# Differential attention's scores in one row-half stretch, and priorities from pool mixer to cross-attention

## The chip, the cores and the metric

The kernel runs on one core of a Trainium2 chip. TensorE (PE in the profile) multiplies matrices: it loads a stationary operand (a weight load, PEld) and streams columns past it into a bank of PSUM, the accumulator memory. VectorE (DVE), ScalarE (ACT) and GpSimd (POOL) work on the elements, SyncE (SP) and POOL issue the transfers (DMA). Each engine runs its own instructions in their order; semaphores make one wait for another. The metric is device microseconds of one execution; less is better.

## The reference, cut to what matters

Two decoder layers over 512 tokens of 1024 features. Each layer: half-step SwiGLU feed-forward, token mixer, cross-attention into 256 memory tokens, second half-step feed-forward, each followed by a residual layer norm. The mixer of layer 0 is differential attention, that of layer 1 a causal pooling mixer.

```python
def block(args):                       # differential attention, 128 queries
    qblk, i = args
    s = jnp.einsum('bqhcd,bkhcd->bhcqk', qblk, k).astype(jnp.float32) * scale
    qpos = i * DA_QBLOCK + jnp.arange(DA_QBLOCK)
    mask = kpos[None, :] <= qpos[:, None]
    s = jnp.where(mask, s, jnp.finfo(jnp.float32).min)
    p = jax.nn.softmax(s, axis=-1)
    a = p[:, :, 0] - lam * p[:, :, 1]
    return jnp.einsum('bhqk,bkhe->bqhe', a.astype(v.dtype), v)
...
for i in range(DEPTH):
    m, j = i % N_MIXERS, i // N_MIXERS
    x = layer_norm(a * x + 0.5 * swiglu_ffn(x, ffn_w_in[i, 0], ffn_w_out[i, 0]), ln_g[i, 0], ln_b[i, 0])
    ...                                # h: differential attention or pool mixer
    x = layer_norm(a * x + h, ln_g[i, 1], ln_b[i, 1])
    x = layer_norm(a * x + memory_cross_attention(x, mem, xa_wq[i], xa_wkv[i], xa_wo[i]), ln_g[i, 2], ln_b[i, 2])
    ...
```

There are eight heads. A head has two maps (c = 0, 1) with 64 features each for queries and keys, and 128 features for values. Query block i of 128 tokens sees (i + 1) x 128 keys.

## The kernel before, in words

**Numbers.** Every float32 operand is split into a high part and a low rest, both in a 32-bit format that TensorE reads fast. A product is three matrix products: high by high, low by high, high by low. `split` makes the high part on ScalarE and the rest on VectorE; `mm3` issues the three products and returns an estimated time, 3 x max(107, 0.42 x columns) ns, which drives the weaving below.

**Order.** The program is written as a sequence of instructions; a planner lays it out on the engines ahead of time. Among instructions that it holds ready on an engine it takes the one written first, unless a block is under `high_priority`. `issue_after` and `after` put an instruction behind a named one of its engine. `weave` runs a main generator and a side generator: the main one reports the estimated time of its products, and when that time reaches the gap (900 ns here) times the weight that the side last returned, the side may write its next step. `WAIT` makes the side ask again.

**Differential attention (`diff_attention`).** Main (`da_main`) projects queries and keys of each head (`q`, `k`; 24 products of 512 columns each) and, per two heads, values (`v`), then multiplies the first four heads' results by the output weights. Side (`da_side`) does the attention itself, in four blocks of queries a head. Step s writes the scores of block s (`da_scores`), the mixture of block s - 1 (`da_mix`), its transposes for block s - 2 (`da_turn`), the output of block s - 3 (`da_out`), and, at the end of a head, the scale (`da_scale`) and its turn (`da_turn_out`). A head's scores may begin 6000 ns of main time after its keys are written.

**Scores.** Queries and keys of a head lie as 128 rows: map 0 in rows 0 to 63, map 1 in rows 64 to 127. For blocks 0 and 1, `da_key` copies the first 256 keys on ScalarE into tiles that hold zeros in the other half's rows (`low`, line 1139), so that one product with all 128 rows yields both maps side by side (line 1154). For blocks 2 and 3 each map is a product of 64 rows, alternating between the halves (line 1159). Per map, VectorE masks and reduces (line 1164) and ScalarE takes the exponential (line 1167).

**Banks.** [...] Two (`mm`) serve the projections; six (`aux`: px, py, yz, two each) rotate through the scores, transposes and outputs. The output of two blocks shares a bank: ScalarE copies a part out (line 1205), VectorE adds the other (line 1206), and two squares on ScalarE write into the bank again as scratch (line 1209).

**Pool mixer to cross-attention (layer 1).** `pool_mixer` splits the tokens, pools them by band matrices (`pp`), multiplies by group weights (`ps`) and ends with the layer norm (`ln_token`: square on ScalarE, line 379, variance, line 380, power on POOL, line 381, two passes on VectorE, lines 383 and 385). It is the side of a weave whose main part (`early_kv`) computes keys and values of the memory for the first heads of cross-attention (`pk`, `pv`). Its first keys' weights come from `cols`, whose splits appear under lines 125 and 126. `xa_main` then projects the queries (`xq`) in two halves of 256 tokens, because the last tokens' transposes (`turn_late`, `pt`, line 496) come late.

Of the kernel before, what the change touches and what calls it, by code (L numbers as in the profile page):

```python
# [9 lines left out]
F32 = mybir.dt.float32  # L10
# [7 lines left out]
P = 128  # L18
D = 1024
S = 512  # L20
# [18 lines left out]
W_SC, W_T, W_O, W_E = (1.1, 1.4, 1.8, 2.2), (0.5, 0.7, 0.9, 1.1), (0.4, 0.8, 0.6, 1.1), (0.6, 0.8)  # L39
LM, LT, LO, LS = 1, 2, 3, 5  # L40
# [69 lines left out]
class Trunk:  # L110
# [1020 lines left out]
    def da_key(self, ps):  # L1131


        k, t = self.pair("qk"), self.da_rope(ps)
        apart = self.keys_apart[len(self.heads) % 2]
        self.split(k[0], k[1], t)
        for whole, part in zip(k, apart):
            for m, rows in enumerate(HALVES):
                self.nc.scalar.copy(part[rows, m], whole[rows, : 2 * P].bitcast(F32))
        return k, apart  # L1140

    def da_scores(self, st, i):

        nc = self.nc
        q, k, n = st["q"], st["k"], (i + 1) * P
        qi, kn = slice(i * P, n), slice(0, n)
        mx, rc, cf = self.small("mx"), self.small("rc", (P, 1)), self.small("cf", (P, 1))
        sm = st["sm"][:, i]
        mm, terms = nc.tensor.matmul, ((0, 0), (1, 0), (0, 1))
        if i < 2:  # L1150
            both = self.aux("sc")[:, : 2 * n].rearrange("p (m n) -> p m n", m=2)
            sc = [both[:, m] for m in range(2)]
            for a, b in terms:
                mm(both, q[a][:, qi], k[1][b][:, :, kn], start=a == b, stop=b == 1)
        else:
            sc = [self.aux("sc")[:, :n] for m in range(2)]
            for a, b in terms:
                for m, rows in enumerate(HALVES):
                    mm(sc[m], q[a][rows, qi], k[0][b][rows, kn], start=a == b, stop=b == 1)
        p = [self.tmp("p")[:, :n] for m in range(2)]  # L1160
        with self.tc.high_priority():
            for m in range(2):
                least = mx[:, m : m + 1]
                nc.vector.tensor_tensor_reduce(
                    p[m], sc[m], self.mask[:, S - n :], -1.0, -NEG, ALU.add, ALU.min, least
                )
                nc.scalar.activation(
                    p[m], p[m], AF.Exp, bias=least, scale=-1.0, accum_out=sm[:, m : m + 1]
                )
        st["m", i] = p, sm, rc, cf  # L1170
# [93 lines left out]
    def da_side(self):  # L1264

        n = DA_H * NT
        for s in range(n + LS + 2):
            h, i = divmod(s, NT)
            if s < n:
                while h >= len(self.heads) or self.clock < self.heads[h][0] + LEAD:  # L1270
                    yield WAIT
                self.da_scores(self.heads[h][1], i)
                yield W_SC[i]
            h, i = divmod(s - LM, NT)
            if 0 <= s - LM < n:
                self.da_mix(self.heads[h][1], i)
            h, i = divmod(s - LT, NT)
            if 0 <= s - LT < n:
                self.da_turn(self.heads[h][1], i)
                yield W_T[i]  # L1280
            h, i = divmod(s - LO, NT)
            if 0 <= s - LO < n:
                while len(self.heads[h][1]["v"]) < NT:
                    yield WAIT
                self.da_out(self.heads[h][1], i)
                yield W_O[i]
            h, i = divmod(s - LS, NT)
            if 0 <= s - LS < n and i == NT - 1:
                self.da_scale(self.heads[h][1])
                yield W_E[0]  # L1290
            h, i = divmod(s - LS - 1, NT)
            if 0 <= s - LS - 1 < n and i == NT - 1:
                self.oT[h] = self.da_turn_out(self.heads[h][1])
                yield W_E[1]

    def diff_attention(self, layer, ln):
        self.keys_apart = [self.pair("low", (P, 2, 2 * P)) for i in range(2)]
        for pair in self.keys_apart:
            for t in pair:
                for m, rows in enumerate(HALVES):  # L1300
                    self.nc.gpsimd.memset(t[rows, 1 - m].bitcast(F32), 0.0)
# [56 lines left out]
    def pool_mixer(self, layer, ln):  # L1358
# [39 lines left out]
        for t in range(NT):  # L1398
# [17 lines left out]
            self.ln_token(t)  # L1416
# [344 lines left out]
```

## Time and profile before

| | |
|---|---|
| Median of three runs | 1916.96 us (1916.87 to 1918.63) |
| Profiled execution, its own time | 1915.99 us |
| Its span, first to last instruction | 1914.2 us |
| TensorE busy | 1898.0 us, 99% |
| VectorE, ScalarE, GpSimd busy | 1551.7, 1016.6, 319.3 us |
| Mean granted TensorE clock | 0.999 |
| Differential attention | some 344 to 555 us of the span |
| Pool mixer to the first queries of cross-attention | some 1386 to 1460 us |

Rows in order of time give start, duration, engine, line, operation, output <- inputs, the operands' shape, how many were merged, and in brackets how long the engine stood idle before and what released it. Matrix products overlap in the array, so a row's duration is longer than the time after which the next one starts; what a product costs is read from start to start. In the rows that group instructions, the numbers after the bar are total busy time, mean ns of one, and idle time just before them.

### The profile page before, as it was taken

How to read it: one execution, taken by the hardware profiler on the slowest of the kernel's cores; microseconds unless marked ns; L12 is line 12 of the kernel's file. 1: busy time of each engine (PE TensorE's matmuls, PEld its weight loads, DVE VectorE, ACT ScalarE, POOL GpSimd, SP SyncE). 2: the span in 40 equal slices, each digit the busy share in tenths (PEclk: the TensorE clock that was granted, in tenths of full speed). 3: DMA queues.
4: the chain of work that ended last, by engine and by line, in shares of the span. 5: the costliest groups of instructions: out<-in, count | busy, mean ns of one | idle time of the engine just before them, and what ended most of it. 6: DMA issues, size and time to landing. Idle time of an engine off the chain costs nothing.

```text
span 1914.2 us, 32507 instructions
## 1 busy us (share of the span) xinstructions
PE 1898.0 (99%) x13088; PEld 1732.0 (90%) x13088; DVE 1551.7 (81%) x2250; ACT 1016.6 (53%) x1578; POOL 319.3 (17%) x282
## 2 busy tenths in 40 slices
PE   9999999999999999999999999999999999999998
PEld 8999998888879888999998999999898889999996
DVE  7888889888867558889888988898787568998886
ACT  6555454566745435655553655555455436555552
POOL 3112121111110002221220311212130012211210
PEclk9999999999999999999999999999999999999999
DMA  9978772332225317987785687878344438867861
GB/s 249 215 176 177 177 139 78 91 89 67 89 67 161 116 60 194 193 175 164 143 191 171 117 180 166 181 164 186 101 132 133 137 84 174 178 156 168 189 130 54
DMA packets 246743, 277.96 MB, mean 145 GB/s; under 512 B 8256, under 2 KB 212544, under 8 KB 246592
## 3 DMA queue, kind: packets, MB, share of 16 engines
q0 software_dynamic: 92928, 92.29, 31.5%
q1 hardware_dynamic: 153664, 183.59, 29.9%
q8 instruction: 103, 1.69, 0.4%
q14 instruction: 48, 0.39, 0.1%
HBM read 273.75 MB, written 2.10 MB: 144 GB/s over the span
## 4 chain that ended last, share of the span: by engine, by line
PE 82%; DVE 11%; ACT 3%; DMA 2%; issue 1%; POOL 1%; SPq 0%; DVEq 0%; ACTq 0%; POOLq 0%
PE x L210 7%; PE x L211 7%; PE x L212 7%; PE z L210 4%; PE z L211 4%; PE z L212 4%; PE ps L210 4%; PE ps L212 4%; PE ps L211 4%; PE px L212 2%; PE px L210 2%; PE px L211 2%; PE y L212 2%; PE y L210 2%; PE y L211 2%; PE pz L212 1%
## 5 line engine op out<-in xcount | busy, mean ns | idle before, releaser
L715 POOL DMA_DIRECT2D ra<-in_ffn_w_in_dram x132 | 170.8, 1316 | 981.8 <-DVE wl L722 966.2
L720 ACT CAST wh<-ra 128x1024 fp32r<-128x1024 f32 x176 | 185.1, 1054 | 206.9 <-PE x L211 65.7
L722 DVE TENSOR_TENSOR wl<-ra,wh 128x1024 fp32r<-128x1024 f32 x176 | 214.2, 1222 | 66.5 <-ACT wh L720 66.1
L210 PE MATMUL x<-xe,wh 128*128 128x256 f32 x704 | 194.8, 277 | 0.0
L211 PE MATMUL x<-xe,wh 128*128 128x256 f32 x704 | 194.6, 276 | 0.0
L212 PE MATMUL x<-xe,wl 128*128 128x256 f32 x704 | 194.5, 276 | 0.0
L720 ACT CAST wh<-rc 128x1024 fp32r<-128x1024 f32 x132 | 138.9, 1053 | 101.6 <-PE x L211 41.4
L125 ACT CAST wh<-b 128x1024 fp32r<-128x1024 f32 x112 | 117.8, 1051 | 130.5 <-PE x L211 67.2
L722 DVE TENSOR_TENSOR wl<-rc,wh 128x1024 fp32r<-128x1024 f32 x132 | 160.0, 1220 | 24.9 <-ACT wh L720 24.9
L126 DVE TENSOR_TENSOR wl<-b,wh 128x1024 fp32r<-128x1024 f32 x112 | 136.8, 1221 | 40.2 <-ACT wh L125 40.2
L210 PE MATMUL x<-xh,wh 128*128 128x256 f32 x536 | 148.5, 277 | 0.0
L211 PE MATMUL x<-xl,wh 128*128 128x256 f32 x536 | 148.2, 276 | 0.0
L212 PE MATMUL x<-xh,wl 128*128 128x256 f32 x536 | 148.2, 276 | 0.0
L211 PEld LDWEIGHTS x<-xe,wh 128*128 128x128 f32 x704 | 132.3, 188 | 1.4
L210 PEld LDWEIGHTS x<-xe,wh 128*128 128x128 f32 x704 | 132.1, 188 | 1.3
L212 PEld LDWEIGHTS x<-xe,wl 128*128 128x128 f32 x704 | 132.2, 188 | 0.0
L126 DVE TENSOR_TENSOR wl<-raw,wh 128x1024 fp32r<-128x1024 f32 x64 | 82.2, 1288 | 42.0 <-ACT wh L125 41.2
L211 PEld LDWEIGHTS x<-xl,wh 128*128 128x128 f32 x536 | 100.7, 188 | 0.7
L210 PEld LDWEIGHTS x<-xh,wh 128*128 128x128 f32 x536 | 100.6, 188 | 0.7
L212 PEld LDWEIGHTS x<-xh,wl 128*128 128x128 f32 x536 | 100.6, 188 | 0.0
L125 ACT CAST wh<-raw 128x1024 fp32r<-128x1024 f32 x64 | 66.4, 1048 | 60.6 <-PE xq L211 20.2
L210 PE MATMUL z<-xe,wh 128*128 128x256 f32 x352 | 97.4, 277 | 0.0
(451 smaller groups left out, 6289.7 us busy)
## 6 DMA issues: line engine op xcount, KB each, us to landing
ra<-in_ffn_w_in_dram POOLq DMA_DIRECT2D x132, 512.0 KB, 6.9
rc<-in_ffn_w_in_dram SPq DMA_DIRECT2D x88, 512.0 KB, 5.9
b<-in_ffn_w_out_dram SPq DMA_DIRECT2D x76, 512.0 KB, 4.8
ra<-in_ffn_w_in_dram SPq DMA_DIRECT2D x44, 512.0 KB, 5.0
rc<-in_ffn_w_in_dram POOLq DMA_DIRECT2D x44, 512.0 KB, 7.5
raw<-in_xa_wkv_dram SPq DMA_DIRECT2D x16, 1024.0 KB, 5.4
raw<-in_da_w_qkv_dram SPq DMA_DIRECT2D x16, 512.0 KB, 5.2
raw<-in_xa_wq_dram SPq DMA_DIRECT2D x8, 1024.0 KB, 5.2
```

The source lines that it names most:

```text
L125: self.nc.scalar.copy(hi, src),
L126: self.nc.vector.tensor_sub(lo, src, hi.bitcast(F32)),
L210: self.first_mm = mm(out, w[0], x[0], start=start, stop=False, skip_group_check=again)
L211: mm(out, w[0], x[1], start=False, stop=False, skip_group_check=again)
L212: self.last_mm = mm(out, w[1], x[0], start=False, stop=stop, skip_group_check=again)
L715: nc.gpsimd.dma_start(t, source(*block), accum_op=ALU.add)
L720: hi = nc.scalar.copy(v[0], raw)
L722: lo = nc.vector.tensor_sub(v[1], raw, v[0].bitcast(F32))
```

## The change

- `da_scores` writes the scores of all four blocks at once, in the order 1, 0, 2, 3, each map as products of 64 rows. It takes all six rotating banks; blocks 0 and 2 share two of them. The masks and exponentials of all four blocks follow, still under priority.
- The apart copies of the keys (`keys_apart`), their ScalarE copies and the clearing of their tiles on GpSimd are gone.
- `da_side` runs one head after the other in a fixed list of steps with new weights; the turn of the previous head's result stands behind the next head's scores. A head's mixture tiles (`p`) grow from six to eight.
- In the pool mixer, the norm of the last token (t = 3) is under priority.
- In `xa_k`, the splits of the first early keys' weights are under priority.
- In `xa_main`, the last waiting token is turned after four of the eight steps of the second product instead of after all eight.

```diff
+W = dict(scores=2.0, turn=(1.0, 1.0, 1.2, 1.5), out=(0.6, 0.8, 1.2, 2.0), scale=0.8, last=0.8)
+STEPS = (
+    ("mix", 1), ("mix", 0), ("mix", 2), ("turn", 0), ("mix", 3), ("turn", 1),
+    ("out", 0), ("turn", 2), ("out", 1), ("turn", 3), ("out", 2), ("out", 3),
+)
+SC_ORDER = (1, 0, 2, 3)
...
-        for whole, part in zip(k, apart):
-            for m, rows in enumerate(HALVES):
-                self.nc.scalar.copy(part[rows, m], whole[rows, : 2 * P].bitcast(F32))
-        return k, apart
+        k = self.pair("qk")
+        self.split(k[0], k[1], self.da_rope(ps))
+        return k
...
-        if i < 2:
-            both = self.aux("sc")[:, : 2 * n].rearrange("p (m n) -> p m n", m=2)
-            for a, b in terms:
-                mm(both, q[a][:, qi], k[1][b][:, :, kn], start=a == b, stop=b == 1)
...
+        one, two, three = ([self.aux("sc") for m in range(2)] for i in range(3))
+        banks = {
+            0: [t[:, 3 * P :] for t in two],
+            1: [t[:, : 2 * P] for t in one],
+            2: [t[:, : 3 * P] for t in two],
+            3: three,
+        }
+        for i in SC_ORDER:
+            qi, kn = slice(i * P, (i + 1) * P), slice(0, (i + 1) * P)
             for a, b in terms:
                 for m, rows in enumerate(HALVES):
+                    mm(banks[i][m], q[a][rows, qi], k[b][rows, kn], start=a == b, stop=b == 1)
+        for i in SC_ORDER:
...
+        for h in range(DA_H):
+            while h >= len(self.heads) or self.clock < self.heads[h][0] + LEAD:
+                yield WAIT
+            st = self.heads[h][1]
+            self.da_scores(st)
+            yield W["scores"]
+            if h:
+                self.oT[h - 1] = self.da_turn_out(self.heads[h - 1][1])
+                yield W["last"]
+            for step, i in STEPS:
+                if step == "out":
+                    while len(st["v"]) < NT:
+                        yield WAIT
+                getattr(self, "da_" + step)(st, i)
+                if step != "mix":
+                    yield W[step][i]
+            self.da_scale(st)
+            yield W["scale"]
...
-            self.ln_token(t)
+            with self.tc.high_priority() if t > 2 else nullcontext():
+                self.ln_token(t)
...
-            with self.after(self.x_split if raw and not then else ()):
+            with self.tc.high_priority() if then else self.after(self.x_split if raw else ()):
                 wk = self.cols(rk, j)
...
-                    yield from self.project(ps[c], ws[c], (p,))
-                    self.turn_late(max(len(self.late) - 1, 0) if c == 0 else 0)
+                    for k, ns in enumerate(self.project(ps[c], ws[c], (p,))):
+                        yield ns
+                        if c and k == 3:
+                            self.turn_late()
+                    if c == 0:
+                        self.turn_late(max(len(self.late) - 1, 0))
...
-            bufs = dict(low=4, rt=2, a=4, p=6, o=2, qk=8, _x=0, v=4, oT=11, mask=1)
+            bufs = dict(low=4, rt=2, a=4, p=8, o=2, qk=8, _x=0, v=4, oT=11, mask=1)
```

More of the change, by code (lines that the diff above doesn't have):

```diff
@@ L38 @@
 V_FIRST, LEAD, GAP = 6, 6000, 900
-W_SC, W_T, W_O, W_E = (1.1, 1.4, 1.8, 2.2), (0.5, 0.7, 0.9, 1.1), (0.4, 0.8, 0.6, 1.1), (0.6, 0.8)
-LM, LT, LO, LS = 1, 2, 3, 5
+W = dict(
+    scores=2.0,
+    turn=(1.0, 1.0, 1.2, 1.5),
+    out=(0.6, 0.8, 1.2, 2.0),
+    scale=0.8,
+    last=0.8,
+)
+STEPS = (
+    ("mix", 1), ("mix", 0), ("mix", 2), ("turn", 0), ("mix", 3), ("turn", 1),
+    ("out", 0), ("turn", 2), ("out", 1), ("turn", 3), ("out", 2), ("out", 3),
+)
+SC_ORDER = (1, 0, 2, 3)
 HALVES = (slice(0, DA_DK), slice(DA_DK, P))
@@ L1157, in da_scores @@
             for a, b in terms:
                 for m, rows in enumerate(HALVES):
[L1159 to L1169, printed above, removed]
@@ L1170, in da_scores @@
-        st["m", i] = p, sm, rc, cf
+                    mm(banks[i][m], q[a][rows, qi], k[b][rows, kn], start=a == b, stop=b == 1)
+        for i in SC_ORDER:
+            n = (i + 1) * P
+            mx, rc, cf = self.small("mx"), self.small("rc", (P, 1)), self.small("cf", (P, 1))
+            sm = st["sm"][:, i]
+            p = [self.tmp("p")[:, :n] for m in range(2)]
+            with self.tc.high_priority():
+                for m in range(2):
+                    least = mx[:, m : m + 1]
+                    nc.vector.tensor_tensor_reduce(
+                        p[m], banks[i][m], self.mask[:, S - n :], -1.0, -NEG, ALU.add, ALU.min, least
+                    )
+                    nc.scalar.activation(
+                        p[m], p[m], AF.Exp, bias=least, scale=-1.0, accum_out=sm[:, m : m + 1]
+                    )
+            st["m", i] = p, sm, rc, cf
@@ L1264, in da_side @@
     def da_side(self):
[L1266 to L1294, printed above, removed]
@@ L1296, in diff_attention @@
-    def diff_attention(self, layer, ln):
[L1297 to L1301, printed above, removed]
+        for h in range(DA_H):
[16 more added lines that the diff above has]
+            yield W["scale"]
@@ L1302, in diff_attention @@
+        self.oT[h] = self.da_turn_out(st)
+        yield W["last"]
+    def diff_attention(self, layer, ln):
         self.mask = self.act("mask", (P, S), mybir.dt.bfloat16)
```

14 lines of the change are left out of this document (2 added, 12 removed).

## The prediction

> **What bounds the kernel now.** I read the head of the page first, then the stretches of the two stages that the change touches, then who waits for whom, then single instructions of these stages in order of time. The page's busy times and the view by stretches of time (columns: busy time of PE, weight loads, DVE, ACT and POOL with their counts, clock, DMA share, GB/s):
>
> ```profile
> PE 1898.0 (99%) x13088; PEld 1732.0 (90%) x13088; DVE 1551.7 (81%) x2250; ACT 1016.6 (53%) x1578; POOL 319.3 (17%) x282
> ...
> 440.00:460.00 20.00, 20.00 (x103) 15.68 (x102) 16.88 (x44) 12.22 (x32) 4.26 (x6) 1.00 0.20 54
> 1386.00:1412.00 26.00, 25.04 (x176) 22.96 (x176) 22.85 (x27) 13.15 (x21) 13.41 (x8) 1.00 0.48 162
> 1440.00:1470.00 30.00, 28.61 (x232) 27.11 (x231) 21.57 (x26) 15.06 (x22) 1.37 (x2) 1.00 0.58 179
> ```
>
> TensorE is busy 1898.0 of 1914.2 us, at full clock. In differential attention (440 to 460) it has no idle time at all while VectorE is busy 16.9 of 20 us. So there the time is the sum of what TensorE is given, and an instruction less on it is time gained as long as the others keep up. Around the pool mixer it idles a little: 0.96 us in 1386 to 1412 and 1.39 us in 1440 to 1470. What it waits for there is told by two rows of the view of waits (engine, line, waited for: total, times, longest):
>
> ```profile
> PE pk L212 <- DVE wl L126: 1.0, 3, 0.4
> PE pt L496 <- DVE X L385: 0.9, 2, 0.7
> ```
>
> These are the low parts of the early keys' weights and the end of a token's norm, the two things that get priority. So all three targets exist; the first is long work on the bound engine, the other two are small waits.
>
> **Part 1, the scores.** Before, blocks 0 and 1 of a head multiply all 128 rows by keys that lie apart with zeros (line 1154); both maps come out of one product, twice as many columns. Blocks 2 and 3 use row halves (line 1159), each in a stretch of its own. In order of time, blocks 0 and 1 of the first head, then block 2 and block 3 of a later one:
>
> ```profile
> 368.95 0.51 PE L1154 MATMUL sc<-low,qk 128*128 128x256 f32 x3
> 369.30 0.40 PE L210 MATMUL k<-xh,wh 128*128 128x512 f32 x1
> ...
> 370.00 0.85 PE L1154 MATMUL sc<-low,qk 128*128 128x512 f32 x3
> 370.69 0.40 PE L210 MATMUL k<-xh,wh 128*128 128x512 f32 x1
> ```
> ```profile
> 443.13 0.39 PE L212 MATMUL q<-xh,wl 128*128 128x512 f32 x1
> 443.45 0.79 PE L1159 MATMUL sc<-qk 64*128 64x384 f32 x6
> 444.18 0.50 PE L210 MATMUL k<-xh,wh 128*128 128x512 f32 x1
> 444.51 0.40 PE L211 MATMUL k<-xl,wh 128*128 128x512 f32 x1
> ```
> ```profile
> 447.64 0.39 PE L211 MATMUL k<-xl,wh 128*128 128x512 f32 x1
> 447.87 0.40 PE L212 MATMUL k<-xh,wl 128*128 128x512 f32 x1
> 448.19 0.96 PE L1159 MATMUL sc<-qk 64*128 64x512 f32 x6
> 449.08 0.50 PE L210 MATMUL k<-xh,wh 128*128 128x512 f32 x1
> 449.42 0.40 PE L211 MATMUL k<-xl,wh 128*128 128x512 f32 x1
> ```
>
> Durations overlap in the array, so I count from start to start. An ordinary 512-column product takes 0.233 us (447.64 to 447.87), that is 0.117 for 256 columns and 0.175 for 384. Block 0 costs 369.30 - 368.95 = 0.35 us, block 1 0.69 us. For block 2 I take 443.13 to 444.51, 1.38 us, less the two ordinary products in it: 1.38 - 0.47 = 0.91 us. Its six products are three pairs; if the halves of a pair run side by side they need 3 x 0.175 = 0.53, so 0.38 us go on entering and leaving the half mode. Block 3: 1.55 - 0.47 = 1.08, less 3 x 0.233, again 0.38. That both sizes leave the same rest says that halves do run side by side and that a stretch costs 0.38 us whatever is in it. One head: 0.35 + 0.69 + 0.91 + 1.08 = 3.03 us.
>
> After, one stretch holds all four blocks in three pairs each, and pays 0.38 once. Blocks 1, 2, 3 cost 3 x (0.117 + 0.175 + 0.233) = 1.58. Block 0 has pairs of only 128 columns, and no half-row pair under 384 columns is in the trace. Its bounds: by columns alone 3 x 0.058 = 0.17; above, by how fast new weights can come. The attention output shows that:
>
> ```profile
> 441.02 0.33 PE L1199 MATMUL po<-v,a 128*128 128x256 f32 x1
> 441.19 0.22 PE L1200 MATMUL po<-v,a 128*128 128x128 f32 x1
> 441.25 0.33 PE L1199 MATMUL po<-v,a 128*128 128x256 f32 x1
> ```
> ```profile
> 448.19 0.53 PEld L1159 LDWEIGHTS sc<-qk 64*128 64x128 f32 x6 [0.36 <-issue]
> ```
>
> A 256- and a 128-column product with weights of their own take 0.23 us together, 0.115 each, where columns alone would be 0.175: a fresh load costs 0.115 us. Six half-row loads one behind the other would start over 5 x 0.115 = 0.58 us, yet all six of block 3 lie within 0.53 us to the end of the last, so the two loads of a pair go side by side. I take 0.115 a pair, 3 x 0.115 = 0.35. If loads were serial after all, blocks 0 and 1 would cost 3 x 0.23 each, 1.38 in place of 0.70. So a head costs 0.38 + 0.35 + 1.58 = 2.31 us, between 2.13 and 2.99; the saving is 0.72, between 0.90 and 0.04; over eight heads 5.8 us, between 7.2 and 0.3.
>
> [...]
>
> The ScalarE copies that make the apart keys go:
>
> ```profile
> L1139 ACT CAST low<-qk 64x256 fp32r<-64x256 f32 x32 | 12.9, 404 | 1.1 <-DVE qk L126 0.7
> ```
>
> 12.9 us less on an engine that is busy 12 of 20 us: nothing on the path, since TensorE covers it, though it shortens the way from key to scores. The clearing of those tiles on POOL goes too, at nothing, behind TensorE.
>
> **Part 2, what the stretch adds.** Six banks are taken at once, all that exist beside the two of the projections. The bank that comes free last is that of the previous head's second pair of outputs. How long one is held, in order of time, for such a pair (last product, copy, add, last square):
>
> ```profile
> 496.53 0.22 PE L1200 MATMUL po<-v,a 128*128 128x128 f32 x1
> 497.32 0.36 ACT L1205 COPY o<-po 128x256 f32<-128x256 f32 x1
> 499.27 0.42 DVE L1206 TENSOR_TENSOR o<-o,po 128x256 f32<-128x256 f32 x1
> 500.75 0.19 ACT L1209 ACTIVATION_READ_ACCUMULATOR po<-o 128x1 f32 x1
> ```
>
> From the last product's start and 0.06 us for its columns, 496.59, to 500.94 it is 4.35 us. In the new order, outputs of block 3 are followed by weights of 2.0 + 0.8 = 2.8, times the gap of 900 ns: 2.5 us of main work on a clock that counts 645 ns for three 512-column products which take 0.70, so 2.7 us. Block 3, which needs that bank, comes last in the stretch, after 0.19 (half of the switch) and 3 x (0.117 + 0.115 + 0.175) = 1.22 us. Free at 4.35, wanted at 4.1: a coin toss. If it isn't free, the order of TensorE was laid out with other work in between, and the stretch splits at 0.38 us more. By the same clock a head's k follows the last head's by 10.3 us inside a pair and by 20.6 across pairs; a head asks for 12.9 x 0.9 = 11.6 us. So scores wait for the head itself in two of seven changes and follow directly in five. Bounds: 0, and 5 x 0.38 = 1.9 us; I take the half, 1.0, since want and supply are that close. What is queued behind the waiting product on TensorE is the projections, which VectorE's rotation then waits for; that case is a rival below. The bursts of eight reductions and eight exponentials with priority I cost at nothing: they were there, cover is the projections' work of 5.6 us per 24 products, and VectorE had 3 of 20 us free.
>
> **Part 3, early keys' weights.** TensorE in order of time, then VectorE:
>
> ```profile
> 1394.69 0.39 PE L212 MATMUL pk<-mem0h,wl 128*128 128x256 f32 x1 [0.45 <-DVE wl L126]
> ...
> 1398.13 0.39 PE L212 MATMUL pk<-mem0h,wl 128*128 128x256 f32 x1 [0.34 <-DVE wl L126]
> ```
> ```profile
> 1391.61 1.28 DVE L385 SCALAR_TENSOR_TENSOR X<-X,rstd,sr 128x1024 f32<-128x1024 f32 x1 [0.44 <-POOL rstd L381]
> ...
> 1393.41 1.22 DVE L126 TENSOR_TENSOR wl<-raw,wh 128x1024 fp32r<-128x1024 f32 x1
> ```
>
> TensorE idles 0.45 and 0.34 us before the first products with low parts: 0.8 us to win. Going first, the first low part (now at 1393.41) fits into the 0.44 us in which VectorE waits and pushes the norm (L385) back by about 0.8. That norm is late next: the split of its token and then the pool products hang on it, so part of the 0.8 comes back there as a wait. Bounds: 0.8 won, and 0.8 lost; I take 0.5 won, because the matrix products of values stand between as filler.
>
> **Part 4, the last token's norm and its turn.** TensorE in order of time, then ScalarE and VectorE:
>
> ```profile
> 1452.49 1.09 PE L496 MATMUL pt<-ident,X 128*128 128x128 f32 x8 [0.74 <-DVE X L385]
> 1453.82 0.50 PE L210 MATMUL xq<-xh,wh 128*128 128x256 f32 x2 [0.24 <-ACT xh L125]
> 1454.55 0.38 PE L211 MATMUL xq<-xl,wh 128*128 128x256 f32 x1 [0.23 <-DVE xl L126]
> ```
> ```profile
> 1446.00 0.19 ACT L379 ACTIVATION_READ_ACCUMULATOR sq<-X,mean 128x1 f32 x1
> ...
> 1447.52 0.22 ACT L380 ACTIVATE var<-var 128x1 f32<-128x1 f32 x1
> ...
> 1448.83 1.27 DVE L383 SCALAR_TENSOR_TENSOR X<-X,mean,gb 128x1024 f32<-128x1024 f32 x1
> ...
> 1451.16 1.28 DVE L385 SCALAR_TENSOR_TENSOR X<-X,rstd,gb 128x1024 f32<-128x1024 f32 x1
> ```
>
> The variance stands 1.33 us behind the square (1446.19 to 1447.52) and the last step 1.06 behind the first (1450.10 to 1451.16), both behind splits of weights and other tokens. With priority the token is ready some 2.4 us earlier, near 1450.0. The turn moves up by four steps of three 256-column products, 1.4 us, from 1452.5 less the wait of 0.74, 1451.7, to 1450.3: just met. The three waits, 0.74 + 0.24 + 0.23 = 1.21 us, can go, and with them some restart; I take 1.2, between 1.4 and a loss of 0.3, if the token comes 0.3 late and a split that was pushed back is missed. The turn's evictions now lie under the four steps left behind it.
>
> **Sum.** 5.8 - 1.0 + 0.5 + 1.2 = 6.5 us. The profiled execution took 1915.99 us (span 1914.2 and 1.8 around it), so 1909.5; the median of the runs, 1916.96, is 0.97 above it: 1910.5.
>
> **Rivals.** *Loads of a pair are serial*: part 1 gives 0.3 instead of 5.8, the total 1.0, so 1916.0; the single row of six loads speaks against it. *The pool side gives nothing or a little back*: 5.8 - 1.0 - 0.8 = 4.0, so 1913.0; for it speaks that the norm pushed back has its own followers, against it that the waits name exactly what is moved. *Banks*: TensorE's order was laid out as if the bank were free and the product then stands and waits on ScalarE's squares. With 4.35 us held and up to 2 us more when a burst of exponentials is ahead of the squares, 2 us for each of seven changes is 14 us lost against 5.8 + 0.5 + 1.2 = 7.5 won: 1923.5. It decides from 7.5 / 7 = 1.1 us a change. For it: all six banks; against it: every bank of the present order goes through the same steps, and TensorE has no idle time in the stretch quoted. [...]
>
> **How the numbers follow.** My forecast 0.62, the pool side giving nothing 0.13, serial loads 0.08, banks 0.17. 0.2% is 3.8 us, about what a measurement can tell from no change. Faster 0.75 (the pool rival loses 4.0 and just counts), same 0.08, slower 0.17. Best case of all bounds: 7.2 + 0.8 + 1.4 = 9.4, 1907.6; a little beyond it 1906.5. Above, the range takes in the serial loads and ends at 1917.5, which leaves the banks out. The forecast's own range is 1906.5 to 1912.5.
>
> **What would show it.** Right: products of 64x128 and 64x256 beside the others in one stretch of 24, about 2.3 us from the ordinary product before to the one after; eight stretches and no more; TensorE still at 20 of 20 us in that stage; the attention stage some 5 us shorter; no waits of pk on L126 and of pt on L385 around 1390 and 1450. Wrong: pairs of block 0 at 0.23 us, stretches in two pieces, waits of sc on ScalarE's square, or VectorE's rotation late so that projections wait for their bank.

## The result and the profile after

The changed kernel took 1939.43 us (median of four runs, 1937.20 to 1941.36) against 1917.09 for the kernel before beside it: a ratio of 1.0115 (95% interval 1.0103 to 1.0127), slower by 22 us. The forecast was 1910.5, faster. The profiled execution is one of 1941.36 us, with a span of 1939.6.

The page's busy times, and the view by stretches of time (the columns as in the prediction) of the changed kernel: first the whole attention stage, then pieces of ten us in it:

```profile
PE 1904.8 (98%) x13136; PEld 1741.5 (90%) x13136; DVE 1552.8 (80%) x2250; ACT 1006.3 (52%) x1546; POOL 317.6 (16%) x274
```
```profile
344.00:608.00 264.00, 242.98 (x1438) 204.69 (x1436) 190.33 (x467) 136.91 (x358) 39.96 (x53) 0.95 0.23 71
380.00:390.00 10.00, 10.00 (x72) 9.77 (x71) 6.63 (x14) 4.00 (x10) 1.28 (x1) 0.84 0.14 45
...
500.00:510.00 10.00, 6.68 (x27) 5.02 (x26) 8.28 (x31) 7.08 (x22) 1.63 (x3) 0.83 0.12 46
530.00:540.00 10.00, 7.61 (x48) 7.61 (x49) 6.95 (x18) 4.27 (x8) 1.09 (x1) 0.66 0.01 2
```

The same view of the kernel before, over its own attention stage:

```profile
344.00:584.00 240.00, 238.29 (x1398) 198.54 (x1396) 192.45 (x471) 148.61 (x393) 38.53 (x52) 1.00 0.26 80
```

Two things are new. TensorE, idle for 1.7 of 240 us before, is now idle for 21 of 264. And the clock column falls to 0.83 and 0.66 in single pieces. From the first product of values to the first of the early keys the stage took 241.6 us before (337.52 to 579.14) and 267.5 after (340.18 to 607.70). These 25.9 us are the loss. The span of the profiled execution is 25.4 us above that of before: ahead of the stage 2.7 us more passed, behind it 3.2 us less, 1.8 of these in two stretches of the pool side (below).

What TensorE waits for in the changed kernel (engine, line, waited for: total, times, longest):

```profile
PE pt L506 <- DVE p L1185: 17.8, 7, 4.8
PE sc L1162 <- DVE mx L1171: 2.1, 1, 2.1
...
PE pk L222 <- DVE wl L136: 0.6, 2, 0.5
...
PE pt L506 <- DVE X L395: 0.2, 1, 0.2
```

The first row is the largest wait. The last two are what is left of the waits that the pool side was to remove, 1.0 and 0.9 us before. Seven times a first transpose of a mixture (L506) stands and waits for VectorE's mixture (L1185). One head on TensorE, in order of time:

```profile
474.30 2.18 PE L1162 MATMUL sc<-qk 64*128 64x256 f32 x24
476.42 0.50 PE L220 MATMUL k<-xh,wh 128*128 128x512 f32 x1
...
478.62 0.60 PE L506 MATMUL pt<-ident,o 128*128 128x128 f32 x4
...
482.11 0.37 PE L506 MATMUL pt<-ident,p 128*128 128x128 f32 x1 [2.19 <-DVE p L1185]
```

The stretch of 24 is there as forecast. From its end (476.42) TensorE has work for 3.5 us; the turn begins 5.7 us after it. VectorE in the same head:

```profile
476.26 0.41 DVE L1171 CUSTOM_DVE_ANT_0 p<-sc,mask 128x256 f32<-128x256 f32 x1
...
478.25 0.28 DVE L1171 CUSTOM_DVE_ANT_0 p<-sc,mask 128x128 f32<-128x128 f32 x1
...
480.24 0.69 DVE L1171 CUSTOM_DVE_ANT_0 p<-sc,mask 128x512 f32<-128x512 f32 x1
...
481.31 0.74 DVE L1185 SCALAR_TENSOR_TENSOR p<-p,cf 128x256 f32<-128x256 f32 x2
```

The mixtures (L1185) stand behind the reductions (L1171) of all four blocks. The longest wait, in a later head, has more in it. On ScalarE and VectorE, in order of time:

```profile
523.00 1.28 ACT L1235 ACTIVATE o<-o,f 128x128 f32<-128x128 f32 x4 [1.43 <-POOL f L1226]
524.19 0.50 ACT L1174 ACTIVATE p<-p,mx 128x256 f32<-128x256 f32 x1
```
```profile
525.30 0.16 DVE L1183 RECIPROCAL rc<-sd 128x1 f32<-128x1 f32 x1 [3.09 <-ACT p L1174]
...
526.16 0.28 DVE L1171 CUSTOM_DVE_ANT_0 p<-sc,mask 128x128 f32<-128x128 f32 x1
...
531.12 0.69 DVE L1132 TENSOR_TENSOR rt<-rt 128x512 f32<-128x512 f32 x1 [0.93 <-POOL rt L1131]
...
531.99 0.88 DVE L1185 SCALAR_TENSOR_TENSOR p<-p,cf 128x128 f32<-128x128 f32 x2
```

ScalarE waits for GpSimd before it scales the previous head; the new exponentials stand behind that. VectorE waits 3.09 us for them with the reciprocal that begins the mixture of block 1, and the reductions of blocks 0, 2 and 3 stand behind it. Then the mixtures stand behind a rotation that waits for GpSimd. TensorE meanwhile:

```profile
527.20 0.44 PE L506 MATMUL pt<-ident,p 128*128 128x128 f32 x2
532.39 0.47 PE L506 MATMUL pt<-ident,p 128*128 128x128 f32 x1 [4.75 <-DVE p L1185]
...
533.73 0.41 PE L222 MATMUL v<-wh,xl 128*128 128x256 f32 x1
533.94 0.41 PE L220 MATMUL v<-wh,xh 128*128 128x256 f32 x1
```

The two last rows show the second loss: products of 256 columns start 0.21 us apart, where before the wait they start 0.12 apart. The clock record has six such stretches at half clock in this stage, five of 3.41 us and one of 6.83, 23.9 us in all.

The account of the stage: waits of 20.9 us in all, less 1.4 that the kernel before has there, 19.5 us; 23.9 us at half clock, of which 2.3 were waits already counted, so half of 21.6, 10.8 us; 1.3 us because the last head's stretch came in two pieces (the price of that is read below, in the spread kernel); less 5.8 us saved in the stretches. That gives 25.8 of the 25.9 measured.

### The profile page after: what moved, and what is told of

Read it like the earlier page. It is cut to its first block, busy times and chain, and to the rows that moved or that the text cites. A ratio compares the mean times of both kernels' runs of the same rounds, so it can differ in the third digit from the quotient of the medians.

```text
span 1939.6 us, 32560 instructions
## 1 busy us (share of the span) xinstructions
PE 1904.8 (98%) x13136; PEld 1741.5 (90%) x13136; DVE 1552.8 (80%) x2250; ACT 1006.3 (52%) x1546; POOL 317.6 (16%) x274
## 4 chain that ended last, share of the span: by engine, by line
PE 81%; DVE 11%; ACT 3%; DMA 2%; issue 1%; POOL 1%; SPq 0%; DVEq 0%; POOLq 0%; ACTq 0%
PE x L220 7%; PE x L221 7%; PE x L222 7%; PE z L220 4%; PE z L221 4%; PE z L222 4%; PE ps L220 4%; PE ps L221 4%; PE ps L222 4%; PE px L220 2%; PE px L222 2%; PE px L221 2%; PE y L222 2%; PE x L757 2%; PE y L220 2%; PE y L221 2%
```

## The experiments

Ratios are to the kernel before on the same chip, with 95% intervals. Where an expectation names theories A, B or C, the letters hold for that expectation alone.

**The first turn later.** The weight behind the scores, 2.0 in the changed kernel, is the room that TensorE has before the first turn.

```diff
-    scores=2.0,
+    scores=5.0,
```

> The changed kernel with the weight of the scores 5.0 in place of 2.0, so that the first turn of a head is written 2.7 us of the main clock later; order and banks are else the same. Theory A (TensorE comes to the turn of block 0 some 2.2 us before VectorE has mixed it, and each such wait also halves the clock for 3.4 us): the waits of pt on p (17.8 us) nearly vanish, the granted clock is back at 0.999, and the time is that of the kernel before less 5.8 us (scores) and 1.8 us (pool side): 1909.5, up to 1912 if the last head's side has no main work beside it at the end. Theory B (VectorE can't keep up with eight reductions at once): the waits move to later turns, the total of waits stays above 12 us, 1930 or more. Theory C (six banks at once): the scores wait for banks, as the last head does, no matter where the turn stands; 1925 to 1940.

1926.82 us, ratio 1.0061 (1.0046 to 1.0076). The attention stage fell from 267.5 to 252.9 us, and the profiled execution, the fastest of the four at 1922.44 us, had no half clock in that stage; the other three, 1926.08 to 1928.98 us, show a mean granted clock of 0.997 against its 0.999. Waits:

```profile
PE po L1207 <- DVE a L136: 6.3, 7, 2.2
PE pt L506 <- DVE p L1185: 3.8, 4, 1.2
PE sc L1162 <- DVE mx L1171: 2.3, 1, 2.3
```

Theory A asked for 1909.5 to 1912 us, so this is a miss for it. The place of the first turn is a large part of the loss, but waits of 14.2 us are left in the stage, and nearly half of them moved on to the outputs (po), which stand next in the same row of steps.

A weight of 3.5 between the two:

```diff
-    scores=2.0,
+    scores=3.5,
```

> The same with the weight 3.5. The changed kernel has 3.3 us of other TensorE work between the scores and the first turn, and the mix is ready some 5.7 us after the scores; this has 4.7 to 5.0. Theory A: waits of 0.7 to 1.0 us a head remain, 5 to 8 us in all, too short to halve the clock (the two of 1.58 us in the changed kernel did not): 1909.5 + 6 = 1916. Theory B and C: as with 5.0, no fall below 1930.

1935.09 us, 1.0109 (1.0093 to 1.0124): a miss for A, in the range of B and C. Five waits for the mixture with 13.7 us remain, the longest of 5.0. More room does not shorten the waits in proportion.

**Filler in front of the turn.** Nine useless products of 512 columns, which the reference does not have, are written into the first turn's bank ahead of it.

```diff
-        pt = self.aux("pt").rearrange("p (c n) -> p c n", c=NT)
+        bank = self.aux("pt")
+        if i == 0:
+            for _ in range(9):
+                self.nc.tensor.matmul(bank, st["q"][0][:, :P], st["k"][0], start=True, stop=True)
+        pt = bank.rearrange("p (c n) -> p c n", c=NT)
```

> The changed kernel with nine more 512-column products ahead of each head's first turn, into the bank of the turn, which the transposes then overwrite: 2.1 us of useless work a head, 16.8 us in all, in the place of the wait. Theory A with the clock as a second loss (half the clock for 3.4 us follows a wait of 2.3 us or more): waits fall below 4 us in all, the clock stays at 0.999, and in spite of the added work the time falls by the 12 us that the half clock cost: about 1927. If the clock does not hang on the waits: no change or slower, 1939 to 1945, with the dips still there.

1943.06 us, 1.0148 (1.0133 to 1.0164). Of six stretches at half clock one was left, of 6.8 us (mean granted clock 0.997, against 0.993 in the changed kernel), behind the one long wait that was left:

```profile
PE pt L506 <- DVE p L1185: 6.9, 3, 4.7
```

So the half clock here follows the waits and is no property of the row halves. The time was missed: 72 products of 0.233 us are 16.8 us, and they stood in place of 9.1 us of waits (20.9 in all before, 11.8 now, 1.8 of them new at the outputs). With 17.1 us less at half clock, 8.5 us, that would still be a gain of 0.8 us; the stage took 268.1 us, 0.6 more than in the changed kernel. By the ratios the kernel is some 6 us slower than the changed one, more than the profiled executions differ; what took the rest stays open.

**A lighter VectorE.** The low parts of the query and key weights are left out (the high part stands in their place, which changes the numbers), so that VectorE has 173.5 instead of 190.3 us to do between 344 and 608 us.

```diff
-            for q in range(2):
-                self.last_low = nc.vector.tensor_sub(
-                    lo[:, :, q], src[:, :, q], hi[:, :, q].bitcast(F32)
-                )
-        return w
+        return w[0], w[0]
```

> The changed kernel without the low parts of the weights of queries and keys: the high part is used in their place, so the result is less exact, TensorE's work is the same, and VectorE is spared 3.2 us a head (two times 0.8 us for each of two weight tiles), some of it in the midst of the burst. If VectorE's lateness sets the waits: those of pt on p fall by more than half, to below 8 us, and the time by 12 us or more, to 1927 or less. If banks or ScalarE's exponentials set them: waits within 3 us of 17.8, 1936 to 1941.

1938.73 us, 1.0119 (1.0105 to 1.0133), the time of the changed kernel, with the same waits:

```profile
PE pt L501 <- DVE p L1180: 16.8, 7, 4.8
```

One of the splits that are left out had stood between the reductions of the head shown above (0.68 us at 477.65). In the same head without it, VectorE mixes block 1 there, after 0.30 us of waiting for an exponential, and the first turn still begins 5.5 us after the stretch, against 5.7. So 9% less load on VectorE does not help. Whether the order of the burst does is what the next two runs test.

**The order of the burst.** The reductions of blocks 2 and 3 go behind the mixture of block 0:

```diff
             st["m", i] = p, sm, rc, cf
+            if i == 0:
+                with self.tc.high_priority():
+                    self.da_mix(st, 1)
+                    mixed = self.da_mix(st, 0)
...
-            with self.tc.high_priority():
+            with self.tc.high_priority(), self.tc.issue_after(mixed.ins) if i > 1 else nullcontext():
```

> The changed kernel, with the mixes of blocks 1 and 0 written between the reductions, and the four reductions of blocks 2 and 3 (2.8 us of VectorE) put behind the mix of block 0. TensorE's order stays (3.3 us of work between scores and first turn). Theory A (the first turn comes too early for the burst): block 0 is mixed some 2.2 us earlier, so the waits of pt on p fall from 17.8 to below 6 us, the clock stays near 0.999, 1917 to 1922. Theory B (VectorE is behind as a whole in the burst): the waits move to the turns of blocks 2 and 3 or to the outputs, at least 12 us stay in all, above 1928.

1931.01 us, 1.0076 (1.0062 to 1.0090). The waits for the mixture fell from 17.8 to 7.7 us, and 3.3 us of waits for ScalarE's copies came up at the outputs. Theory A's time (1917 to 1922) was missed: 14.4 us of waits are left in the stage and some 10 us at half clock, as theory B said. But the order is worth some 7 us.

The other queue: the previous head's scale goes behind the new exponentials on ScalarE, its turn behind the third turn, with a weight of 2.6 behind the scores.

```diff
+                if h and (step, i) == ("turn", 1):
+                    with self.tc.issue_after(self.last_exp.ins):
+                        self.da_scale(self.heads[h - 1][1])
+                    yield W["scale"]
+                if h and (step, i) == ("turn", 2):
+                    self.oT[h - 1] = self.da_turn_out(self.heads[h - 1][1])
+                    yield W["last"]
```

> The changed kernel, with the scale of the previous head's output put behind the new head's exponentials on ScalarE, and its turn behind the new head's third turn; the weight of the scores is 2.6, so that the first turn keeps its 2.5 to 3.3 us behind the scores. In the longest wait of the changed kernel (4.75 us, at 532) the exponentials stood behind that scale, which waited for POOL. If that place in the queue is a cause: that wait and the one of the sixth head shrink to the 2.3 us of the others, the waits of pt on p fall from 17.8 to 10 to 14 us, the scores of the last head come in one piece, ratio 1.005 to 1.008. If it is not: ratio 1.010 or more, waits of 16 us or more.

1927.51 us, 1.0060 (1.0046 to 1.0074): no wait for the mixture over 2.5 us, three stretches at half clock, and the last head's stretch whole. In all, the waits for the mixture fell less than expected, to 14.9 us instead of 10 to 14; the rest of the gain is time at half clock, 10.2 us instead of 23.9. Since the two longest waits are gone, what the longest one showed, exponentials behind a scale that waits for GpSimd, is a cause beside the order of the reductions and the place of the turn. The scale, the turn and the weight were moved together here, so what each is worth alone isn't shown.

**Together.** A weight of 5.0 with the mixture first:

```diff
-    scores=2.0,
+    scores=5.0,
```

> The changed kernel with both earlier edits: weight 5.0 for the scores, and the reductions of blocks 2 and 3 behind the mix of block 0. Alone the first left 15 us of waits in the attention stage (turns, outputs, and one of scores on a bank), the second 16 us. If both work on the same chain (scores to the first mixed block to the first turn) and their gains add: waits of 6 to 9 us, 2.4 of them the bank of the last head, no half clock, and the time near that of the kernel before, ratio 0.998 to 1.001. If the time that the mix wins is lost again at the outputs: waits above 12 us, ratio 1.004 or more.

1937.79 us, 1.0113 (1.0099 to 1.0126): the second of the two expectations, the gains do not add. The waits stand at the outputs (6.5 and 4.9 us) and come two or three close together, and 23.9 us at half clock are back.

All three, with a weight of 4.5:

```diff
-    scores=2.0,
+    scores=4.5,
```

> All three edits of the order together, with weight 4.5: the reductions of blocks 2 and 3 behind the mix of block 0, the previous head's scale behind the exponentials, its turn later, the first turn 4.2 to 4.9 us behind the scores. If the changed kernel loses by the places of its steps alone, the 5.8 us of the scores and the 1.8 us of the pool side come out nearly whole: waits below 5 us, ratio 0.996 to 0.998. If the burst itself is too long for any place: waits of 8 us or more, ratio 1.000 or more.

1920.95 us, 1.0024 (1.0013 to 1.0035): some 17 of the 22 us are back, but not the rest. Some 8 us of waits are left in the stage, 4.5 at the outputs and 1.9 at the scores, and 6.8 us at half clock. In each of these kernels, where one head's steps stand behind one burst, another step waited next.

**The parts alone.** The kernel before, with blocks 0 and 1 also in row halves, each block in a stretch of its own:

```diff
-            for a, b in terms:
-                mm(both, q[a][:, qi], k[1][b][:, :, kn], start=a == b, stop=b == 1)
+        for a, b in terms:
+            for m, rows in enumerate(HALVES):
+                mm(sc[m], q[a][rows, qi], k[0][b][rows, kn], start=a == b, stop=b == 1)
```

> The kernel before with blocks 0 and 1 in row halves too, but each block in a stretch of its own and in the old order of steps: four switches a head in place of two; the keys' copies on ScalarE fall away as far as nothing reads them (they are still made). If a switch costs 0.38 us: block 0 goes from 0.35 to 0.38 + 0.35, block 1 from 0.69 to 0.38 + 0.35, 0.42 us a head, 3.4 us in all, 1920.5. If switches hide beside other work: 1917 or less. No new waits in either case.

1919.90 us, 1.0026 (1.0016 to 1.0035). Stage +4.4 us, of which 1.0 are waits; 3.4 us over eight heads, 0.43 a head, agree with the prices of the prediction (two switches of 0.38 more, 0.34 saved in the products).

The kernel before with the three edits of the pool side and of cross-attention alone:

```diff
+            with self.tc.high_priority() if t > 2 else nullcontext():
+                self.ln_token(t)
...
+            with self.tc.high_priority() if then else self.after(self.x_split if raw else ()):
...
+                        if c and k == 3:
+                            self.turn_late()
```

> The kernel before with the pool side of the change alone (priority for the last token's norm and for the first early keys' weights, the turn four steps earlier). In the changed kernel the stretch from the first early keys to the pool products is 0.31 us shorter than before, and that of the first queries 1.45 us. If these are this part's own doing: 1.8 us faster, ratio 0.9991. If they come from the later arrival of the stage in the changed kernel: within 0.5 us of before.

1914.07 us, 0.9987 (0.9978 to 0.9996): faster than before, by 2.4 us. The first queries' stretch went from 20.92 to 19.60 us, the early keys' from 11.58 to 11.26.

Two stretches a head, blocks (0, 1) and (2, 3), in the old order of steps, with the pool side:

```diff
+        if i == 0:
+            both = [self.aux("sc") for m in range(2)]
+            banks = {0: [t[:, 3 * P :] for t in both], 1: [t[:, : 2 * P] for t in both]}
+        else:
+            banks = {j: [self.aux("sc")[:, : (j + 1) * P] for m in range(2)] for j in (2, 3)}
```

> The pool side of the change, and scores in row halves in two stretches a head, blocks 0 and 1 together and blocks 2 and 3 together, in the old order of steps with one step between scores and mix; no apart keys, eight tiles p. By the measured prices: 2 x 0.38 for switches, 0.35 + 0.35 + 0.53 + 0.70, so 2.69 us a head against 3.03, 2.7 us in all; VectorE's bursts are of four reductions, 1.7 and 2.8 us. If the burst of eight was the trouble: no new waits, ratio 0.9977 (2.7 + 1.8 us). If any bunching of the reductions makes TensorE wait: more than 5 us of waits, slower than before.

1914.50 us, 0.9993 (0.9984 to 1.0002). By the prices the stage should have been 2.7 us shorter; it was 1.1 longer. Waits, for example of transposes for a bank that a reduction still reads, explain 1.0 us of that (2.4 us in the stage against 1.4 before); 2.8 us stay open.

**One stretch, the burst spread out.** The stretch of 24 in the old order of steps: the reductions and exponentials of blocks 0 and 1 follow it, those of blocks 2 and 3 come with the next two steps. The pool side is as changed.

```diff
-                self.da_scores(self.heads[h][1], i)
+                if i == 0:
+                    self.da_scores(self.heads[h][1])
+                    self.da_soft(self.heads[h][1], 0)
+                    self.da_soft(self.heads[h][1], 1)
+                elif i < 3:
+                    self.da_soft(self.heads[h][1], i + 1)
```

> One stretch of 24 products per head as in the changed kernel, the pool side as changed, but the old order of steps behind it: the reductions and exponentials of blocks 0 and 1 follow the stretch, those of block 2 and of block 3 come with the next two steps, and the last two transposes and outputs of the previous head lie between. Theory A, the long stretch is worth what was forecast (5.8 us) and what was lost is the burst of eight reductions and eight exponentials ahead of the first turn: no wait of transposes for the mixture over 1 us, waits of TensorE in the attention stage under 3 us, no stretch of time at half clock, the stage 235 to 239 us, ratio 0.995 to 0.998. Theory B, taking six banks at once is itself the cost, since the previous head's transposes and outputs need them right behind the stretch: waits of transposes or outputs for a bank or an exponential of 5 us or more, the stage over 244 us, ratio 1.000 or more.

1937.56 us, 1.0108 (1.0091 to 1.0125): the time that B expected and a miss for A, but the wait is neither's. TensorE and VectorE in order of time:

```profile
467.78 2.17 PE L1152 MATMUL sc<-qk 64*128 64x128 f32 x21
469.88 0.51 PE L210 MATMUL k<-xh,wh 128*128 128x512 f32 x1
473.16 1.49 PE L1152 MATMUL sc<-qk 64*128 64x512 f32 x3 [2.78 <-DVE mx L1163]
```
```profile
473.03 0.08 DVE L1163 DVE_READ_ACCUMULATOR2_ANT mx<- 128x1 f32 x1
```

The last three products of the stretch, the second map of block 3, stand apart and wait until the reduction of block 2's first map is done (473.11). In the old order the output of block 0 is written ahead of the next head's scores, and its bank is held until that of block 1 follows behind them. So five banks are free, not six, and the sixth is taken from block 2. TensorE waits 8.2 us so, five times; transposes wait for the mixture once, 0.6 us, as A said. The split itself costs too, here where nothing waits:

```profile
386.82 0.28 PE L211 MATMUL v<-wl,xh 128*128 128x256 f32 x1
387.21 0.96 PE L1152 MATMUL sc<-qk 64*128 64x512 f32 x3
388.09 0.39 PE L212 MATMUL v<-wh,xl 128*128 128x256 f32 x1
388.32 0.28 PE L210 MATMUL v<-wh,xh 128*128 128x256 f32 x1
```

From 386.82 to 388.32 are 1.50 us, less two products of 256 columns (0.23) 1.27 us. The piece of 21 takes as long as a whole stretch, 2.31 us, since the three products of the other half that would have run beside it are missing. So a split is 1.27 us more, and seven of eight stretches are split here: some 8.9 us.

Next, the same with that bank set free: outputs of blocks 0 and 1 go together, behind the next head's stretch, with some more weight there.

```diff
-            if 0 <= s - LO < n:
+            if 0 <= s - LO < n and i:
                 while len(self.heads[h][1]["v"]) < NT:
                     yield WAIT
+                if i == 1:
+                    self.da_out(self.heads[h][1], 0)
                 self.da_out(self.heads[h][1], i)
```

> As the spread kernel, but no output bank is held over the stretch: the output of block 0 is written together with that of block 1, behind the next head's stretch, so that six banks are free for it; and one unit of weight more lies behind the stretch. Theory A, what the changed kernel loses is the burst ahead of the first turn, and the stretch itself is worth what was forecast: all eight stretches of 24 products whole, waits of TensorE in the attention stage under 3 us, no stretch of time at half clock, the stage 235 to 239 us, ratio 0.995 to 0.998. Theory B, with six banks taken at once something always waits behind the stretch: waits of transposes, outputs or scores of 5 us or more, the stage over 244 us, ratio 1.000 or more.

1914.97 us, 0.9997 (0.9988 to 1.0006): 22.6 us less than with the bank held, neither theory's time. The weights behind the steps changed too (the first from 1.1 to 2.0), so the 22.6 us are not the bank's alone. All eight stretches are whole in TensorE's order, and no transpose waits for a mixture any more; the stage is 244.2 us. What is left is mainly bank waits inside two stretches, one of them followed by 6.8 us at half clock:

```profile
476.93 0.95 PE L1152 MATMUL sc<-qk 64*128 64x128 f32 x12
478.67 1.03 PE L1152 MATMUL sc<-qk 64*128 64x384 f32 x7 [0.79 <-ACT po L1208]
481.51 1.64 PE L1152 MATMUL sc<-qk 64*128 64x512 f32 x5 [1.80 <-DVE a L126]
```

Here the wait on ScalarE's squares is in sight that the prediction's bank rival named (L1208), and another on the eviction of a transpose. Last, more room ahead of the stretch:

```diff
-W_SC, W_T, W_O, W_E = (2.0, 1.4, 1.6, 1.9), (0.5, 0.7, 0.9, 1.1), (0.4, 0.8, 0.6, 1.1), (0.6, 0.8)
+W_SC, W_T, W_O, W_E = (1.7, 1.4, 1.6, 1.9), (0.5, 1.9, 0.9, 1.1), (0.4, 0.8, 0.6, 1.1), (0.6, 0.8)
```

> As the spread kernel with six free banks, with one change of place: 1.2 units of weight more between the last turn ahead of the stretch and the stretch, 0.3 less behind it. In the kernel without this, two stretches (at 430 and 477 us) stood for 1.1 and 3.1 us because the eviction of that turn and the squares of an output still held a bank, and 6.8 us at half clock followed the second. Theory A, the stretch is worth the forecast 5.8 us once its six banks are free in time: no wait over 1 us in the attention stage, no stretch of time at half clock, the stage 235 to 238 us, ratio 0.995 to 0.997. Theory B, six banks at once always cost as much as the stretch saves: waits of 3 us or more come back elsewhere, the stage over 241 us, ratio 0.998 or more.

1913.45 us, 0.9982 (0.9973 to 0.9991), faster than both kernels. No half clock is left in the stage:

```profile
344.00:580.00 236.00, 230.04 (x1418) 194.47 (x1417) 192.63 (x468) 133.00 (x357) 39.99 (x51) 1.00 0.26 81
```
```profile
PE pt L496 <- DVE mx L1163: 2.8, 3, 1.6
PE sc L1152 <- DVE a L126: 1.1, 1, 1.1
```

The ratio and the stage are those of theory B, if at its edge: waits came back, the stage is over 241 us. It took 241.1 us, 0.5 less than before, with 5.3 us of waits where the kernel before had 1.4 (the totals of the view of waits over the stage). So without the 3.9 us of new waits it would be some 4.4 us shorter, against the 5.8 of the forecast: the stretch saves most of what it was priced at, and here gives most of that back in waits for the banks that it takes. The interval of the pool side alone (0.9978 to 0.9996) overlaps this one (0.9973 to 0.9991), so it isn't shown that the stretch adds anything to that.

## Why the prediction was wrong

**The step that failed** is the last sentence of part 2: the bursts of eight reductions and eight exponentials "cost at nothing", covered by "the projections' work of 5.6 us per 24 products", since VectorE had 3 of 20 us free. It weighed busy shares. But the burst was a chain on engines that work in their own order (reductions, exponentials, mixtures), 5.7 us from the scores to the first turn in the head shown, and TensorE had 3.5 us of work before that turn. It cost 17.8 us of waits. The kernel with less work for VectorE shows that free time was not the point. Those with a later turn, another order and a later scale show that the length of that chain and the place of the turn matter. The spread kernel with six free banks shows it from the other side: with the same stretch, but half of the burst put off, no turn waits for a mixture, and the time is that of the kernel before.

**Not priced at all** was the clock, 10.8 us. The forecast's full clock was that of a kernel with hardly any waits. What the runs show of it stands in the last section.

**Wrongly sized** was the split. The forecast took 1.0 us for stretches that come in two pieces, five at 0.38 us and half of that. One of eight was split, and a split costs 1.27 us: the sum comes out near, but by luck.

**What was right.** The stretch: 2.31 us a head forecast, 2.31 measured in the seven whole ones. The weight loads of block 0's pairs start 0.111 us apart, two at a time, so pairs are bound by fresh loads about as assumed and rival "serial loads" is out. In detail the pieces shift: block 0 takes 0.29 us instead of 0.35, because its second pair starts 0.06 us behind the first, and the pairs around it take the difference. The switch of 0.38 is confirmed by the blocks in separate stretches. The pool side: 1.7 forecast (0.5 and 1.2), 1.8 found in the changed kernel (0.3 and 1.5) and 1.6 in the same two stretches of the pool side alone; the rival that it gives nothing is out.

**The bank rival** had the right sign, but not the mechanism: in the changed kernel six banks were free in seven of eight heads, and only the last head's stretch split and waited, 2.1 us, for a reduction instead of a square. The demand for six banks acted otherwise: it shaped the order. The old order holds a bank across the stretch (in the spread kernel five waits for a bank, 8.2 us in all, some 8.9 us of splits, and half clock with them), and the changed order, which lets no output lie there, puts a whole head's steps behind one burst.

## What to carry to other kernels

Before matrix work is gathered into one stretch, follow the chain that hangs on it through the in-order engines, in us from the stretch to the first instruction of TensorE that needs its end, and compare that with the work that TensorE has written in between; free shares of VectorE and ScalarE say nothing about it. Ask which banks are held over the place where the stretch takes its own. If a stretch pairs two halves of the array, ask what splits it: here three products parted from their partners cost 1.27 us a head. And look at what stands behind a wait of TensorE: in the changed kernel six of them, of 2.15 us or more and 17.1 us in all, had 23.9 us at half clock with them, 10.8 us lost on top.

## What the runs showed of the hardware

In the attention stage of the changed kernel the record of the clock shows half clock six times: for 3.413 us from 379.86, 431.06, 482.26, 506.16 and 560.77 us of the span, and for 6.827 us from 530.05. The starts lie 15, 15, 7, 7 and 9 times 3.413 us apart. Half clock is also what the products show: those of 256 columns start 0.21 us apart there, 0.12 before.

Beside them, all waits of TensorE of over 0.8 us in that stage, by the idle time that the rows print:

| Wait (us) | Its end | What waited | Half clock |
|---|---|---|---|
| 2.46 | 379.34 | first turn | from 379.86, 3.41 us |
| 1.42 | 400.35 | first turn | none |
| 2.19 | 430.54 | first turn | from 431.06, 3.41 us |
| 1.42 | 452.26 | first turn | none |
| 2.19 | 482.11 | first turn | from 482.26, 3.41 us |
| 3.32 | 505.90 | first turn | from 506.16, 3.41 us |
| 4.75 | 532.39 | first turn | from 530.05, 6.83 us |
| 2.15 | 560.46 | scores | from 560.77, 3.41 us |

Five of the six waits of 2.15 us or more were followed by half clock 0.2 to 0.5 us after their end; in the longest one it had begun 2.3 us before the end. The two of 1.42 us (1.58 in the expectation of the weight 3.5) were not followed by it.

The length of a single wait does not settle it. In the spread kernel with six free banks two shorter waits close together, 0.79 and 1.80 us within one stretch, had half clock behind them: products of 512 columns then start 0.43 us apart (484.10 and 484.52), 0.23 before. In the profiled execution with a weight of 5.0, waits of up to 2.2 and 2.3 us had none, and its mean granted clock is 0.999. So half clock came behind waits of about 2 us in these runs; from which wait on it comes, they do not show.
